# The rotary embedding's transfers on another engine's queue, and the key latent's norm at a later place

## The chip, the cores and the metric

One core of a Trainium2 chip runs the kernel as one program. The metric is the device time of one execution in microseconds. Times are the median of several runs; the profile is one execution taken by the hardware profiler. Five engines have instruction queues of their own and run in order within each: TensorE (PE; its weight loads are shown apart as PEld), VectorE (DVE), ScalarE (ACT), GpSimd (POOL) and SyncE (SP). A transfer is issued by the queue of some engine (shown as SPq or ACTq) and then carried out by the core's 16 DMA engines.

## The reference

Two layers of a decoder trunk over 512 tokens of width 1024, batch 1, all in float32. Each layer normalises its input, projects it with one wide matrix, and feeds three branches: a Mamba-2 state space model, multi-head latent attention (MLA), and a gated delta network. The branches are projected, gated and merged, and a feed-forward block follows. Only the attention branch matters here, in the reference's words:

```python
q = (rmsnorm(cq, q_norm_g) @ w_uq).reshape(Bsz, S, H, MLA_NOPE + MLA_ROPE)
q_nope, q_pe = jnp.split(q, [MLA_NOPE], axis=-1)
q_pe = apply_rope(q_pe, cos[:, :, None, :], sin[:, :, None, :])
kv = (rmsnorm(ckv, kv_norm_g) @ w_ukv).reshape(Bsz, S, H, MLA_NOPE + MLA_V)
k_nope, v = jnp.split(kv, [MLA_NOPE], axis=-1)
k_pe = apply_rope(k_rope, cos, sin)
```

There are 8 heads with 128 plain and 64 rotary columns. The query latent `cq` has 512 columns, the key latent `ckv` 256, and one rotary key of 64 columns serves all heads. `apply_rope` turns the first and second half of the 64 columns into t1 cos - t2 sin and t2 cos + t1 sin. Scores are the sum of the plain and the rotary product; a causal softmax and the product with v follow.

## The kernel before

**Precision.** TensorE multiplies in a rounded format, so each float32 operand is split into a high part (the rounded value) and a low part (the rest), and each product is three matmuls: high x high, high x low, low x high (`mm3`, L180 to L184). The split of a weight tile is a cast on ScalarE (`whi`, L154; L557 and L558 for the query weights) and a subtraction on VectorE (`wlo`, L155; L559 and L560). The split of an evicted result is likewise an operation of ScalarE (L250, L254) and one of VectorE (L251, L255).

**Weights.** They are streamed from HBM by SyncE into the two buffers of `wraw` (L161; L549 for the query weights), 384 or 512 KB at a time. A load is issued when the splits of the load two before are done. The split tiles `whi` and `wlo` have four buffers each, so a cast waits for the matmuls that use the tile four before.

**Order of the work.** The program is written as straight Python; a scheduler then orders the instructions of all engines, mostly as written, with some blocks given a priority. So the place of a statement in the source decides, with its waits, where its instructions stand in each engine's queue. Tiles with the tag `mix` rotate through eight buffers, and one that is written again waits for the last reader of the tile eight before.

**The attention stage of a layer.** A first projection has left the key latent in `ck_tok` (four tiles of 128 tokens x 256) and the rotary key in `kr_tok`. Then, in source order:

- `query_latent(0)` (L494): columns 0 to 255 of the query latent, transposed by construction, as two tiles, evicted with the gain and split (`cqh`, `cql`), and squared (L499, L501).
- `latent(...)` (L472): the key latent's norm and split. ScalarE squares and sums each of the four token tiles (L478). VectorE scales and adds the epsilon (L258), GpSimd raises to the power -1/2 (L259), VectorE multiplies (L482), TensorE transposes eight 128x128 blocks (L487), and the result is split with the gain into `ckh` and `ckl` (L254, L255).
- The rotary key: four transposes (L518), a copy (L520), `rope` (L503), and the split into `kph` and `kps` (L524 to L526).
- `query_latent(1)` (L528): columns 256 to 511 of the query latent.
- The query's norm factors, from column sums (L531).
- Four head pairs (hp 0 to 3). Each computes the queries from `cqh` and `cql` (three tiles: plain queries of two heads, and `qp`, the rotary columns of both; L580), calls `rope(qp)`, swaps its halves through `qd` (L585) and splits into `qps` and `qpl` (casts L589 and L591, subtraction L590). It computes keys (`kh`, `kl`) and values (`vh`, `vl`) from `ckh` and `ckl`, and then for each of the two heads the scores (L622 to L627, of which L625 and L626 are the rotary part), the softmax (L634, L635), transposes (L645) and the product with the values (L661 to L663).

**Transfers of the rotary part.** `rope` needs the tile with its 32-row blocks exchanged in pairs, and moves them within the on-chip memory by four transfers of 64 KB (L507); L585 exchanges the two 64-row halves by two transfers of 128 KB. All these are issued by ScalarE's queue. With five calls of `rope` and four of L585 in each of two layers they are 40 and 16 transfers.

Of the kernel before, what the change touches and what calls it, by code (L numbers as in the profile page):

```python
# [55 lines left out]
def hybrid_kernel(ctx, tc, a, out, depth=2, taps=None):  # L56
    nc = tc.nc
    pe, act, dve, pool, sync = nc.tensor, nc.scalar, nc.vector, nc.gpsimd, nc.sync
    uid = itertools.count()

    def mk(pl, shape, dt, tag, bufs=None):
        return pl.tile(shape, dt, tag=tag, name=f"{tag}_{next(uid)}", bufs=bufs)
# [19 lines left out]
    lp = ctx.enter_context(tc.tile_pool(name="lp", bufs=1))  # L82
# [10 lines left out]
    def sm_bank():  # L93
        return mk(ps_sm, [P, 512], F32, "sm")
# [70 lines left out]
    def weights(w2d, c0, n, K, hold=None, raw0=None):  # L165

        kt = min(1024 // n, K // P)  # L170
        step = 512 // n
        for k0 in range(0, K // P, kt):
            given = raw0 is not None and k0 == 0
            raw = raw0 if given else weights_raw(w2d, c0, n, k0, kt)
            for q in range(0, kt, step):
                hi, lo = split_half(raw[:, q * n : (q + step) * n], hold and hold[k0 + q], not given)
                v = lambda x: x.rearrange("p (k n) -> p k n", n=n)
                yield k0 + q, v(hi), v(lo)
# [7 lines left out]
    def dense_F(gen, cols, K, xh, xl, mid=None, banks=None, after=None):  # L186

        pss = banks or [acc_bank() for _ in cols]
        last = K // P - 1
        if mid:
            gen = list(gen)
            for i, hf in enumerate(HALVES):
                for ps, c in zip(pss, cols):
                    for k0, wh, wl in gen:
                        for k in range(wh.shape[1]):  # L200
                            kk = k0 + k
                            mm3(ps[:, hf], wh[:, k, c], wl[:, k, c], xh[kk][:, hf], xl[kk][:, hf], kk == 0, kk == last)
                if i == 0:
                    mid()
            return pss
        for k0, wh, wl in gen:
            for ps, c in zip(pss, cols):
                for k in range(wh.shape[1]):
                    a_, b_ = wh[:, k, c], wl[:, k, c]
                    mm3(ps[: a_.shape[1], :], a_, b_, xh[k0 + k], xl[k0 + k], k0 + k == 0, k0 + k == last)  # L210
            if after:
                after()
        return pss

    def tiles(n):
        return [slice(i, i + P) for i in range(0, n, P)]
# [36 lines left out]
    def split_gain(hi, lo, ps, g):  # L253
        act.activation(hi, ps, AF.Copy, scale=g)  # L254
        dve.scalar_tensor_tensor(lo, ps, g, f32(hi), ALU.mult, ALU.subtract)  # L255

    def rsq(o, ss, scale, eps, exp=None):
        dve.tensor_scalar(o, ss, scale, eps, ALU.mult, ALU.add)  # L258
        pool.tensor_tensor(o, o, (exp if exp is not None else nhalf)[:, : o.shape[1]], ALU.pow)  # L259
# [5 lines left out]
    def hilo_tags(pl, base, n=KD, w=S):  # L265
        return ([mk(pl, [P, w], F32R, f"{base}h{k}") for k in range(n)],
                [mk(pl, [P, w], F32R, f"{base}l{k}") for k in range(n)])
# [83 lines left out]
    for ly in range(depth):  # L351
# [5 lines left out]
        sconv_b, g_n1, g_ssd, g_q, g_kv, g_gdn, g_n2 = 0, 12, 20, 28, 32, 34, 35  # L357
# [3 lines left out]
        ck_tok = [mk(lp, [P, 256], F32, f"yh{4 + t}") for t in range(T)]  # L361
# [110 lines left out]
        def latent(pl, tok, width, gi, nm):  # L472

            nk = width // P
            ss = mk(sp, [P, T], F32, "lss")
            for t in range(T):
                jk = mk(ml, [P, width], F32, "pn3", 2)
                act.activation(jk, tok[t], AF.Square, accum_out=ss[:, t : t + 1])  # L478
            rs = mk(sp, [P, T], F32, "lrs")
            rsq(rs, ss, 1.0 / width, EPS)  # L480
            for t in range(T):
                dve.tensor_scalar(tok[t], tok[t], rs[:, t : t + 1], None, ALU.mult)  # L482
            hs, ls = hilo_tags(pl, nm, nk)
            for k in range(nk):
                ps = sm_bank()
                for t in range(T):
                    pe.transpose(ps[:, t * P : (t + 1) * P], tok[t][:, k * P : (k + 1) * P], ident)  # L487
                split_gain(hs[k], ls[k], ps, col(gi + k))
            return hs, ls
# [4 lines left out]
        def query_latent(i):  # L494
            for j, ps in enumerate(dense_F(weights(w_in, O_CQ + 256 * i, 256, D), tiles(256), D, xh, xl)):
                k = 2 * i + j
                split_gain(cqh[k], cql[k], ps, col(g_q + k))
                cq_sq.append(mk(ml, [P, S], F32, "pn3", 2))
                act.activation(cq_sq[-1], ps, AF.Square)  # L499
                if k:  # L500
                    dve.tensor_tensor(cq_sq[0], cq_sq[0], cq_sq[k], ALU.add)  # L501

        def rope(src):  # L503

            sw_ = mk(lp, [P, S], F32, "mix", 8)
            for i in range(4):
                act.dma_start(sw_[32 * i : 32 * i + 32], src[32 * (i ^ 1) : 32 * (i ^ 1) + 32])  # L507
            ta = mk(lp, [P, S], F32, "mix", 8)
            dve.tensor_tensor(ta, src, cosT, ALU.mult)
            dve.tensor_tensor(sw_, sw_, sinT, ALU.mult)  # L510
            dve.tensor_tensor(ta, ta, sw_, ALU.add)
            return ta

        query_latent(0)
        ckh, ckl = latent(lp, ck_tok, 256, g_kv, "ck")
        ps = sm_bank()
        for t in range(T):
            pe.transpose(ps[:, t * P : (t + 1) * P], kr_tok[:, t], ident)  # L518
        kd = mk(lp, [P, S], F32, "mix", 8)
        act.copy(kd, ps)  # L520
        kpe = rope(kd)
        kph = mk(ml, [P, S], F32R, "kph")
        kps = mk(ml, [P, S], F32R, "kps")
# [2 lines left out]
        dve.tensor_tensor(kps[64:], kpe[64:], f32(kph[64:]), ALU.subtract)  # L526

        query_latent(1)  # L528
        ps = sm_bank()
        for t in range(T):  # L530
            pe.matmul(ps[:, t : t + 1], cq_sq[0][:, t * P : (t + 1) * P], ones[:, 0:1], start=True, stop=True)  # L531
# [13 lines left out]
        for hp in range(4):  # L545
# [33 lines left out]
            qp = mk(ml, [P, S], F32, "qp")  # L579
            act.mul(qp, pp, scale)  # L580
            qr = rope(qp)

            qd = mk(lp, [P, S], F32, "mix", 8)
            for i in range(2):
                act.dma_start(qd[64 * i : 64 * i + 64], qr[64 * (1 - i) : 64 * (1 - i) + 64])  # L585
            qps = [mk(ml, [P, S], F32R, f"qps{j}") for j in range(2)]
            for j in range(2):
                half, other = (slice(64 * i, 64 * i + 64) for i in (j, 1 - j))
# [715 lines left out]
```

## Time and profile before

| | us |
|---|---|
| median of 3 runs | 2334.94 (2334.29 to 2338.41) |
| the profiled execution | 2335.61 |
| its span in the trace | 2333.8 |
| TensorE busy in the span | 2290.0 |
| VectorE busy | 1585.9 |
| ScalarE busy | 1177.4 |
| 384 KB query weight load, issue to landing (median) | 3.3 |
| 512 KB key/value weight load, issue to landing (median) | 3.7 |
| rotary transfer of 64 KB (L507), issue to landing (median) | 2.0 |
| rotary transfer of 128 KB (L585), issue to landing (median) | 2.3 |

The granted TensorE clock of the profiled execution was 0.996. In rows of the timeline the first number is the start in us from the span's start, the second the duration in us from the first start to the last end of the row's instructions (their number is after the x), and the bracket gives the idle time of that engine before the row and what ended it. A name such as `mix<-qp` is output<-input. Neighbouring matmuls overlap in the trace, so their pace is read from start to start.

### The profile page before, as it was taken

Reading aid. Unit: us, or ns where it says so; the run is one execution under the profiler, and the core shown is the slowest. Engines: PE = TensorE matmul, PEld = TensorE weight load, DVE = VectorE, ACT = ScalarE, POOL = GpSimd, SP = SyncE. Lnnn points to the kernel's source line nnn. Section 1 sums busy time; section 2 is a strip of 40 time slices with the busy share of each in tenths; the row PEclk is TensorE's granted clock in tenths of the full one; section 3 lists DMA queues with packets and bytes.
Section 4 is the critical chain, followed back from the end, with each engine's and each line's share of the span. In section 5 each row is a group of like instructions: output and inputs, shape, how many; then the busy total and the mean of one; then the engine's idle time right before and its main releaser. Section 6 shows DMA issues by size and latency. Waiting matters only on the chain.

```text
span 2333.8 us, 32026 instructions
## 1 busy us (share of the span) xinstructions
PE 2290.0 (98%) x11814; PEld 1884.8 (81%) x11814; DVE 1585.9 (68%) x3116; ACT 1177.4 (50%) x2455; POOL 59.1 (3%) x74
## 2 busy tenths in 40 slices
PE   8999999999999999999999999999999999999998
PEld 7878788878887888888887787888788878888886
DVE  7776666775665458767867765667656645677668
ACT  6666644333443345554656667443334434545545
POOL 0000000000000000000000000000000000000000
PEclk9999999999999999999999999999999999999999
DMA  4223533442222443233132235334422224333231
GB/s 136 83 73 91 171 100 109 122 132 79 80 78 69 148 144 109 74 116 118 51 97 72 74 99 163 105 103 140 115 83 85 68 80 155 127 117 100 91 109 46
DMA packets 208702, 239.85 MB, mean 103 GB/s; under 512 B 33888, under 2 KB 157472, under 8 KB 208544
## 3 DMA queue, kind: packets, MB, share of 16 engines
q1 hardware_dynamic: 205344, 233.07, 33.0%
q10 hardware_dynamic: 3200, 4.72, 0.8%
q8 instruction: 93, 1.52, 0.3%
q14 instruction: 65, 0.53, 0.1%
HBM read 221.41 MB, written 11.63 MB: 100 GB/s over the span
## 4 chain that ended last, share of the span: by engine, by line
PE 88%; DVE 6%; DMA 2%; ACT 2%; POOL 1%; issue 1%; ACTq 0%; SPq 0%; DVEq 0%; POOLq 0%
PE acc L182 23%; PE acc L183 22%; PE acc L184 22%; PE sm L182 2%; PE sm L184 2%; PE sm L183 2%; DVE wlo L155 1%; PE sm L742 1%; DMA eE<-d_c 1%; PE sm L645 1%; DVE tok L858 1%; DVE gQ L857 1%; PE sm L1015 1%; POOL gms L259 1%; PE yt L661 1%
## 5 line engine op out<-in xcount | busy, mean ns | idle before, releaser
L155 DVE TENSOR_TENSOR wlo<-wraw,whi 128x512 fp32r<-128x512 f32 (+1 forms) x552 | 376.5, 686 | 421.7 <-ACT whi L154 407.1
L154 ACT CAST whi<-wraw 128x512 fp32r<-128x512 f32 (+1 forms) x552 | 339.9, 618 | 593.4 <-PE acc L183 384.2
L184 PE MATMUL acc<-xh,wlo 128*128 128x512 f32 (+1 forms) x1248 | 486.3, 390 | 0.0
L182 PE MATMUL acc<-xh,whi 128*128 128x512 f32 (+1 forms) x1248 | 486.0, 390 | 0.0
L183 PE MATMUL acc<-xl,whi 128*128 128x512 f32 (+1 forms) x1248 | 484.6, 389 | 1.0 <-issue 1.0
L184 PEld LDWEIGHTS acc<-xh,wlo 128*128 128x128 f32 x1248 | 235.6, 189 | 45.7 <-issue 1.2
L183 PEld LDWEIGHTS acc<-xl,whi 128*128 128x128 f32 x1248 | 235.7, 189 | 44.2 <-DVE xl L255 0.4
L182 PEld LDWEIGHTS acc<-xh,whi 128*128 128x128 f32 x1248 | 235.2, 189 | 43.7 <-ACT xh L254 0.4
L182 PE MATMUL acc<-yh,whi 128*128 128x512 f32 x384 | 151.9, 399 | 0.0
L183 PE MATMUL acc<-yl,whi 128*128 128x512 f32 x384 | 151.4, 394 | 0.0
L184 PE MATMUL acc<-yh,wlo 128*128 128x512 f32 x384 | 151.2, 394 | 0.0
L686 DVE SCALAR_TENSOR_TENSOR ckl<-acc,pc,ckl 128x511 f32<-128x511 f32 (+2 forms) x168 | 120.2, 743 | 15.5 <-ACT ckl L682 8.2
L154 ACT CAST whi<-wr 128x512 fp32r<-128x512 f32 x128 | 79.5, 621 | 66.6 <-PE acc L184 30.3
L184 PE MATMUL acc<-whi,xl 128*128 128x512 f32 (+1 forms) x288 | 111.3, 386 | 0.0
L183 PE MATMUL acc<-wlo,xh 128*128 128x512 f32 (+1 forms) x288 | 111.1, 386 | 0.0
L182 PE MATMUL acc<-whi,xh 128*128 128x512 f32 (+1 forms) x288 | 110.3, 385 | 0.0
L182 PE MATMUL acc<-whi,yh 128*128 128x512 f32 x256 | 99.7, 390 | 0.0
L184 PE MATMUL acc<-whi,yl 128*128 128x512 f32 x256 | 99.7, 389 | 0.0
L183 PE MATMUL acc<-wlo,yh 128*128 128x512 f32 x256 | 99.6, 389 | 0.0
L155 DVE TENSOR_TENSOR wlo<-wr,whi 128x512 fp32r<-128x512 f32 x128 | 86.0, 685 | 12.2 <-ACT whi L154 11.6
L182 PEld LDWEIGHTS acc<-yh,whi 128*128 128x128 f32 x384 | 71.7, 188 | 16.8 <-ACT yh L254 1.7
L183 PEld LDWEIGHTS acc<-yl,whi 128*128 128x128 f32 x384 | 72.2, 188 | 15.2 <-issue 1.0
(418 smaller groups left out, 4520.9 us busy)
## 6 DMA issues: line engine op xcount, KB each, us to landing
wraw<-in_w_in_dram SPq DMA_DIRECT2D x144, 512.0 KB, 3.6
wraw<-in_w_up_dram SPq DMA_DIRECT2D x64, 512.0 KB, 3.6
wr<-in_w_down_dram SPq DMA_DIRECT2D x32, 1024.0 KB, 5.0
eE<-d_c SPq DMA_DIRECT2D x48, 256.0 KB, 4.0
wraw<-in_w_mla_out_dram SPq DMA_DIRECT2D x16, 512.0 KB, 3.4
eE<-d_e SPq DMA_DIRECT2D x32, 256.0 KB, 3.1
wraw<-in_w_ssd_out_dram SPq DMA_DIRECT2D x16, 512.0 KB, 3.4
wraw<-in_w_gdn_out_dram SPq DMA_DIRECT2D x16, 512.0 KB, 3.4
```

The source lines that it names most:

```text
L154: act.copy(hi, raw)
L155: dve.tensor_tensor(lo, raw, f32(hi), ALU.subtract)
L182: pe.matmul(o, ah, bh, start=start, stop=False, skip_group_check=more)
L183: pe.matmul(o, ah, bl, start=False, stop=False, skip_group_check=more)
L184: pe.matmul(o, al, bh, start=False, stop=stop, skip_group_check=more)
L259: pool.tensor_tensor(o, o, (exp if exp is not None else nhalf)[:, : o.shape[1]], ALU.pow)
L645: pe.transpose(ps[:, n : n + P], pn[t][:, kb * P : (kb + 1) * P], ident)
L661: pe.matmul(o, v_h, th[:, c : c + w], start=kb == 0, stop=False)
L686: dve.scalar_tensor_tensor(acc[:, d:], ps[:, : S - d], taps_[3 - d], acc[:, d:], ALU.mult, ALU.add)
L742: pe.matmul(py[:, h * 64 : (h + 1) * 64], e2[h // 4][:, h % 4, :], xd[:, h * 64 : (h + 1) * 64], start=True, stop=True)
L857: dve.tensor_tensor(pd, bc_last(nb[:, m, m + 1 :], m + 1), bc_mid(xb[:, m, : m + 1], 31 - m), ALU.mult)
L858: dve.tensor_tensor(xb[:, m + 1 :, : m + 1], xb[:, m + 1 :, : m + 1], pd, ALU.add)
```

## The change

The rotary transfers of L507 and L585 are issued by SyncE in place of ScalarE, and the call of `latent` stands behind `query_latent(1)` and no longer behind `query_latent(0)`, so the rotary key's transposes come directly after the first half of the query latent. Nothing else is edited.

```diff
             sw_ = mk(lp, [P, S], F32, "mix", 8)
             for i in range(4):
-                act.dma_start(sw_[32 * i : 32 * i + 32], src[32 * (i ^ 1) : 32 * (i ^ 1) + 32])
+                sync.dma_start(sw_[32 * i : 32 * i + 32], src[32 * (i ^ 1) : 32 * (i ^ 1) + 32])
...
         query_latent(0)
-        ckh, ckl = latent(lp, ck_tok, 256, g_kv, "ck")
         ps = sm_bank()
         for t in range(T):
             pe.transpose(ps[:, t * P : (t + 1) * P], kr_tok[:, t], ident)
...
         query_latent(1)
+        ckh, ckl = latent(lp, ck_tok, 256, g_kv, "ck")
         ps = sm_bank()
...
             qd = mk(lp, [P, S], F32, "mix", 8)
             for i in range(2):
-                act.dma_start(qd[64 * i : 64 * i + 64], qr[64 * (1 - i) : 64 * (1 - i) + 64])
+                sync.dma_start(qd[64 * i : 64 * i + 64], qr[64 * (1 - i) : 64 * (1 - i) + 64])
```

In the changed kernel L518 is L517, L520 is L519, and L524 to L526 are L523 to L525; L507 and L585 keep their numbers.

## The prediction

> **What bounds the kernel now.** I read the page's busy times first, then its chain, then the windows over the attention stages of both layers, and last the timeline of each idle time of TensorE in them.
>
> ```profile
> PE 2290.0 (98%) x11814; PEld 1884.8 (81%) x11814; DVE 1585.9 (68%) x3116; ACT 1177.4 (50%) x2455; POOL 59.1 (3%) x74
> PE 88%; DVE 6%; DMA 2%; ACT 2%; POOL 1%; issue 1%; ACTq 0%; SPq 0%; DVEq 0%; POOLq 0%
> ```
>
> TensorE is busy for 98% of the span and is 88% of the chain of waits. The change takes no matmul away (the built programs have the same ones), so it can win only idle time of TensorE. The order of the built instructions differs between the two kernels only in the latent-attention stage of each layer: about 43 to 200 us and 1199 to 1350 us of the span. Elsewhere every engine has the same sequence. The windows over these stretches, a little wider, end with their sums:
>
> ```profile
> sum 168.00, PE 163.87 PEld 133.48 DVE 133.12 ACT 112.62 POOL 2.06; mean PE 23.41 PEld 19.07 DVE 19.02 ACT 16.09 POOL 0.29
> sum 164.00, PE 157.69 PEld 129.70 DVE 119.97 ACT 104.52 POOL 2.13; mean PE 22.53 PEld 18.53 DVE 17.14 ACT 14.93 POOL 0.30
> ```
>
> 168.00 - 163.87 = 4.13 us idle in layer 0 and 164.00 - 157.69 = 6.31 us in layer 1: 10.4 us in all is the ceiling of any gain, 0.45% of the span. ScalarE (ACT) is busy for 112.62 of 168 us, so it isn't the bound; what counts is only where TensorE waits for it. These are the idle times, in brackets with their releaser:
>
> ```profile
> 54.16 0.44 PE L487 MATMUL sm<-ct,yh 128*128 128x128 f32 x2 [0.88 <-DVE yh L482]
> 82.20 0.50 PE L622 MATMUL sm<-kh,qh 128*128 128x512 f32 x1 [0.37 <-ACT pn L635]
> 144.30 0.39 PE L625 MATMUL sm<-kps,qps 128*128 128x256 f32 x1 [1.46 <-ACT qps L591]
> 152.65 0.50 PE L661 MATMUL yt<-mix,vh 128*128 128x512 f32 x1 [0.81 <-ACT mix L250]
> 153.58 0.50 PE L662 MATMUL yt<-mix,vh 128*128 128x512 f32 x1 [0.44 <-DVE mix L251]
> ...
> 1207.70 0.96 PE L487 MATMUL sm<-ct,yh 128*128 128x128 f32 x6 [1.33 <-DVE yh L482]
> 1230.29 0.47 PE L182 MATMUL acc<-cqh,whi 128*128 128x512 f32 x1 [0.21 <-DVE vl L251]
> 1238.30 0.39 PE L625 MATMUL sm<-kps,qps 128*128 128x256 f32 x1 [2.05 <-ACT qps L591]
> 1302.80 0.39 PE L625 MATMUL sm<-kps,qps 128*128 128x256 f32 x1 [1.31 <-ACT qps L591]
> 1311.15 0.49 PE L661 MATMUL yt<-mix,vh 128*128 128x512 f32 x1 [0.81 <-ACT mix L250]
> 1312.07 0.50 PE L662 MATMUL yt<-mix,vh 128*128 128x512 f32 x1 [0.43 <-DVE mix L251]
> ```
>
> They add up to 10.10 us, nearly the whole ceiling. Two belong to the key latent (L487: 0.88 + 1.33 = 2.21), three to the rotary part of the queries (L625 waiting for qps: 1.46 + 2.05 + 1.31 = 4.82), the rest to the softmax's and the values' evictions.
>
> **Part 1: 56 transfers leave ScalarE's queue for SyncE's.** What an issue costs ScalarE:
>
> ```profile
> L507 ACTq DMA_DIRECT2D mix<-qp x32: 514/601/1077, 68.3 to 1325.3; - x32
> L507 ACTq DMA_DIRECT2D mix<-mix x8: 551/610/621, 57.1 to 1212.6; - x8
> ...
> L585 ACTq DMA_DIRECT2D mix<-mix x16: 501/504/622, 74.8 to 1331.5; - x16
> ```
>
> 32 x 0.601 + 8 x 0.610 + 16 x 0.504 = 32.2 us of ScalarE's queue go. This hides behind TensorE's work except where a ScalarE result is late, so it isn't the gain. The three qps stalls are where it shows. The one of the third head pair, layer 0:
>
> ```profile
> 139.34 0.60 ACT L573 ACTIVATE qh<-acc 128x512 fp32r<-128x512 f32 x1 [0.96 <-PE acc L184]
> 139.93 1.15 ACTq L585 DMA_DIRECT2D mix<-mix  x2
> 141.18 0.62 ACT L154 CAST whi<-wraw 128x512 fp32r<-128x512 f32 x1 [1.24 <-PE acc L183]
> 141.70 1.26 ACT L589 CAST qps<-mix 64x512 fp32r<-64x512 f32 x2
> 142.99 1.26 ACT L591 CAST qps<-mix 64x512 fp32r<-64x512 f32 x2
> ```
>
> The two transfers of L585 can't be issued before the eviction of qh at 139.34, since they stand behind it on ScalarE; only then do the casts L589 and L591 run, and the matmul L625 starts at 144.30, 1.46 late. On SyncE L585 waits only for its data and its buffer, and is issued some 2 us earlier; the 1.15 us of issue is gone from ScalarE, so L589 (1.26) can run from about 139.95, ahead of the cast at 141.18. That cast waits for TensorE's progress and ends near 141.8; the first L591 (0.62) would end near 142.4, and L625 could start at 142.84 = 144.30 - 1.46. The margin is 0.4 us if the data land by 141.8. I take 1.46 - 0.3 = 1.16, and for the same place in layer 1, 1.31 - 0.3 = 1.01: the 0.3 is an estimate, most of the margin, for the landing beside a weight load.
>
> The largest stall, in the first head pair of layer 1:
>
> ```profile
> 1226.29 2.44 ACTq L507 DMA_DIRECT2D mix<-qp  x4
> 1231.82 1.15 ACTq L585 DMA_DIRECT2D mix<-mix  x2
> 1237.63 0.61 ACT L591 CAST qps<-mix 64x512 fp32r<-64x512 f32 x1 [2.71 <-DMA mix<-mix]
> 1232.26 0.37 SPq L161 DMA_DIRECT2D wraw<-in_mla_w_ukv_dram  x1
> 1233.29 0.37 SPq L549 DMA_DIRECT2D wraw<-in_mla_w_uq_dram  x1
> ```
>
> The four L507 block ScalarE for 2.44 us, the value evictions and casts behind them are late, and L585 goes out at 1231.82, when SyncE issues 512 KB at 1232.26 and 384 KB at 1233.29. The second of the two lands only at about 1237.6, and L625 waits 2.05. In the changed order the next pair's key/value load stands ahead of L585 on SyncE, but its wait is for two weight casts that no longer stand behind L507, so it goes out about 2.4 us earlier; L585 then follows it by over 1 us, and the following w_uq load is issued behind L585, not into it. I take all of the 2.05. The 0.21 at 1230.29 (late value evictions behind L507) goes too, and so does the 0.37 at 82.20.
>
> In the other five head pairs qps is no stall. The closest is the fourth of layer 0: L591 starts at 176.27 and its matmul at 176.97 without idle time.
>
> ```profile
> 172.45 1.15 ACTq L585 DMA_DIRECT2D mix<-mix  x2
> 176.27 0.62 ACT L591 CAST qps<-mix 64x512 fp32r<-64x512 f32 x1
> 176.97 0.37 PE L625 MATMUL sm<-kps,qps 128*128 128x256 f32 x1
> ...
> DMA to landing us min/median/max: 2.2/2.3/5.3
> ```
>
> With L585 issued at the same time (172.45) and the usual 2.3 us, it lands by 175.3 and nothing is late; with the 5.3 of the worst one it lands at 178.2, and L625 is about 2 us late. That bound is kept for the range. The median is nearest to seven of the eight pairs, so I cost it at nothing here.
>
> What the moved issues do to SyncE: it issues in order, so a weight load behind L507 or L585 waits for qp or for the rotated tile. An issue there takes 0.37 us (the rows at 1232.26 and 1233.29), 56 of them 20.7 us over 300 us: no bound. The key/value load of the next pair stands behind L507 in the first pair, the w_uq loads and d_c behind it in the second. They are needed a pair later, some 25 us on, and the wait of L507 is for an eviction that is nearly ready when SyncE gets there: nothing.
>
> In the trace the collision at 1232 was between two queues. The Trainium skill ("DMA: Bandwidth & Descriptors", section "Queues, rings and completion order") says that each DMA engine takes turns between the queue rows that have work, packet by packet, and within one row takes descriptors in order. That speaks against the change: a rotary transfer on SyncE would stand behind the whole of a load that it now shares turns with. No row of before shows a small transfer right behind a load on the same queue, so the trace neither bears it out nor refutes it; it is the last rival below.
>
> **Part 2: the key latent moves behind the query latent's second half.** It costs the same instructions at another place; what counts is whether its chain ends before TensorE arrives.
>
> ```profile
> 1203.76 0.42 ACT L478 ACTIVATE pn<-yh 128x256 f32<-128x256 f32 x1 [0.26 <-DVE pn L501]
> ...
> 1205.38 0.42 ACT L478 ACTIVATE pn<-yh 128x256 f32<-128x256 f32 x1
> 1205.92 0.17 DVE L258 TENSOR_SCALAR lrs<-lss 128x4 f32<-128x4 f32 x1 [1.67 <-ACT pn L478]
> 1207.29 1.14 DVE L482 TENSOR_SCALAR yh<-yh,lrs 128x256 f32<-128x256 f32 x4 [1.20 <-POOL lrs L259]
> ...
> 52.53 1.28 ACT L415 ACT_TABLE_LOAD   x1
> 56.48 0.39 PE L184 MATMUL acc<-xh,wlo 128*128 128x512 f32 x1
> 56.71 0.39 PE L182 MATMUL acc<-cqh,whi 128*128 128x512 f32 x1
> 1213.72 0.39 PE L182 MATMUL acc<-cqh,whi 128*128 128x512 f32 x1
> ```
>
> Four squares of 0.54 each (1203.76 to 1205.92) are 2.16 us, the norm's power on GpSimd 1.37 (1205.92 to 1207.29), and the transposes L487 start 0.41 later (1207.70): 3.94 us from the first square. In the changed order the transposes stand behind 32 of the first head pair's query matmuls, at about 0.227 us each (56.48 to 56.71 is one): 7.3 us after the query latent's end. The squares in turn stand on ScalarE behind the evictions of the query latent and five weight casts.
>
> Layer 0: the query latent, which now ends at 56.71, ends without the 0.88 us wait and without the eight transposes ahead of it (about 0.12 each, from 0.96 for six and 0.44 for two): 56.71 - 0.88 - 1.0 = 54.8. TensorE reaches L487 at 54.8 + 7.3 = 62.1. ScalarE has, from the eviction of the half's first tile near 53.6 on, that eviction and the next (0.6 each), the table load (1.28), two squares (0.6 each) and five casts (0.3 to 0.6): 5.9 us by these durations, so the latent's squares start near 59.4, an estimate, and L487 at 59.4 + 3.94 = 63.3: an idle time of 1.2 us in place of 0.88. Layer 1: 1213.72 - 1.33 - 1.0 = 1211.4, arrival 1218.7; there a cast ahead of the squares waits for a matmul of the same stretch, 3.9 us after the query latent's end, which puts the first square at 1215.6 with that cast, and L487 at 1219.5: idle 0.8 in place of 1.33. So 2.0 us in place of 2.21: the stall moves and stays; I cost the move at nothing. Bounds: the whole 2.21 is won if the casts go faster, and 2 us are lost if the eviction of ckh, which then stands behind a cast of the next pair's first w_uq load, has to wait for that load.
>
> The two idle pairs at the third head pair's end (0.81 + 0.44, 0.81 + 0.43) shrink: two 128x256 matmuls of about 0.12 now stand between, 0.24 each, 0.48 in all.
>
> **The sum.** Gains: 1.16 + 1.01 + 2.05 + 0.21 + 0.37 + 0.48 = 5.28; less 1.0 us, an estimate, for rotary transfers that land behind a load at one of the two places with little margin (half of the 2 us above). Net 4.3 us. The profiled execution took 2335.61 us, span 2333.8: 2335.61 - 4.3 = **2331.3 us**. The median of the runs, 2334.94, is 0.67 below the profiled one; I don't subtract that, as the spread of the runs (2334.29 to 2338.41) is larger.
>
> **Rivals.** (a) The latent's stall is gone as well, because ScalarE, free of 32 us of issues, finishes the squares earlier, and no landing is late: 5.28 + 2.21 = 7.5, 2328.1 us. For it: ScalarE is busy for only 67% here. Against: its squares wait for casts that follow TensorE, not for issues. (b) The change doesn't do what it says: the qps stalls are set by the casts' wait for TensorE (the row at 141.18 has 1.24 of it), and come back at L625 in another form: only 0.21 + 0.37 + 0.48 is won, 2334.6 us. (c) Slower: rotary transfers stand in one queue behind a 384 or 512 KB load and take 5.3 us like the worst one now. It decides once the landing passes about 3.5 us, the lead of the third and fourth pairs. Fourth pairs: 2 us late each, in both layers; third pairs: the stall stays and grows by 1.0; the first pair of layer 1 keeps 2.05; the latent loses 2 us on the late w_uq load. 2335.61 + 4.0 + 2.0 + 2.0 - 1.06 = 2342.6 us. By the skill's rule of turns between rows and order within one this is what comes; by the row at 1232, where the landing was 5.3 in a queue of its own, the place of a load matters, not the queue.
>
> **How the numbers follow.** Forecast 0.45 (2329.8 to 2333.0); (a) 0.25; (b) 0.12; (c) 0.18. A measurement of this kernel tells a change from none at about 0.2%, 4.7 us: faster is below 2330.3, slower above 2339.6. The forecast has a ninth of its weight below 2330.3: faster 0.05 + 0.25 = 0.30, plus 0.02 for the edges of (b); same 0.40 + 0.10; slower 0.18. The range reaches from (a) to a half-decided (c): 2327.5 to 2339.0, leaving out 0.05 below and 0.13 above.
>
> **What would show it.** Right: the queue q10 is gone; L507 and L585 stand on SPq at 0.37 each; no L625 row of the third pairs or of 1238 has more than 0.4 idle; L487 has about 1.2 and 0.8. Wrong: L585 landing above 3.5 us, an idle row at L625 in the fourth pairs, ckh's eviction waiting for a DMA, or L487 without idle time (rival a).

## The result, and the profile after

The changed kernel takes 2327.15 us (median of 9 runs, 2322.57 to 2335.17) against 2335.18 for the kernel before (9 runs, 2333.94 to 2338.41): a ratio of 0.9971, 95% interval 0.9961 to 0.9982. That is 4.2 to 9.1 us less. Six further runs gave 0.9968 (0.9955 to 0.9980). The forecast of -4.3 us had the sign and a place in the interval, but about half of the size; the median is just below the range's lower end. The runs of one kernel differ in granted clock (0.992 to 0.999), by about 1.7 us for each 0.001 (the slope over the 70 runs of the kernel before in these comparisons), so kernels are compared below by ratios over many runs and by what TensorE waits for in the two attention stages.

The page after, span, busy times and the transfers' one remaining queue:

```profile
span 2329.9 us, 32047 instructions
PE 2295.1 (99%) x11814; PEld 1891.3 (81%) x11814; DVE 1586.6 (68%) x3116; ACT 1177.7 (51%) x2455; POOL 59.2 (3%) x74
...
q1 hardware_dynamic: 208544, 237.80, 33.5%
```

ScalarE's queue q10 is gone; its 3200 packets are in q1 (205344 before). TensorE's busy time is 5.1 us more for the same matmuls, which fits this execution's lower clock (0.993 against 0.996). The same windows over the two stages as before the prediction end with these sums:

```profile
sum 168.00, PE 165.92 PEld 136.10 DVE 134.50 ACT 114.55 POOL 2.15; mean PE 23.70 PEld 19.44 DVE 19.21 ACT 16.36 POOL 0.31
sum 164.00, PE 161.49 PEld 132.65 DVE 125.21 ACT 109.24 POOL 2.14; mean PE 23.07 PEld 18.95 DVE 17.89 ACT 15.61 POOL 0.31
```

TensorE's idle time is 2.08 + 2.51 = 4.59 us, where it was 10.44. The timeline of TensorE shows what is left (the only rows over 0.2 us):

```profile
63.68 1.22 PE L487 MATMUL sm<-ct,yh 128*128 128x128 f32 x8 [1.11 <-DVE yh L482]
142.22 0.39 PE L625 MATMUL sm<-kps,qps 128*128 128x256 f32 x1 [0.21 <-ACT qps L591]
151.24 0.49 PE L661 MATMUL yt<-mix,vh 128*128 128x512 f32 x1 [0.29 <-ACT mix L250]
152.08 0.50 PE L662 MATMUL yt<-mix,vh 128*128 128x512 f32 x1 [0.35 <-DVE mix L251]
...
1218.18 1.23 PE L487 MATMUL sm<-ct,yh 128*128 128x128 f32 x8 [1.16 <-DVE yh L482]
1264.88 0.39 PE L625 MATMUL sm<-kps,qps 128*128 128x256 f32 x1 [0.53 <-ACT qps L591]
1304.75 0.49 PE L661 MATMUL yt<-mix,vh 128*128 128x512 f32 x1 [0.29 <-ACT mix L250]
1305.59 0.50 PE L662 MATMUL yt<-mix,vh 128*128 128x512 f32 x1 [0.35 <-DVE mix L251]
```

Read against the rows of before: L625's 4.82 us shrank to 0.74; L487's 2.21 became 2.27, so the latent's stall only moved; L661 and L662 shrank from 2.49 to 1.28. These lines account for 5.2 of the 5.85 us of idle time that went, the small rows of before (0.37 and 0.21) for the rest.

The profiled execution of the changed kernel doesn't show the whole gain in its span: 2329.9 against 2333.8 is 3.9 us less. Aligned matmul by matmul (both traces hold 11814), it was 6.5 us ahead of the kernel before at 1310 us and 6.7 at 1620, and fell to 3.4 by 1690, in code that is the same in both. The windows show why; the column before the DMA share is the granted clock. First after, then before:

```profile
55.00:80.00 25.00, 23.89 (x120) 19.76 (x119) 17.56 (x43) 17.37 (x46) 2.15 (x2) 0.93 0.24 74
480.00:520.00 40.00, 38.13 (x356) 30.53 (x354) 27.71 (x62) 14.78 (x26) 0.00 (x0) 0.87 0.51 132
1640.00:1680.00 40.00, 38.70 (x459) 31.09 (x458) 24.45 (x54) 17.04 (x29) 0.00 (x0) 0.87 0.48 120
```

```profile
55.00:80.00 25.00, 25.00 (x136) 20.85 (x135) 18.59 (x42) 14.89 (x37) 1.01 (x1) 1.00 0.34 97
480.00:520.00 40.00, 38.12 (x359) 30.89 (x358) 29.32 (x65) 15.09 (x25) 0.00 (x0) 0.89 0.52 136
1640.00:1680.00 40.00, 37.82 (x464) 30.69 (x463) 30.40 (x67) 15.86 (x27) 0.00 (x0) 1.00 0.51 133
```

The clock doesn't dip at the same places in every execution; here three dips more fell on the profile of after (the two shown, and one at 11 us). In another profile of the changed kernel no dip fell ahead of the last matmul. There the same matmuls of the attention stages, the 194th to the 1151st and the 5941st to the 7001st of the trace, took 2.94 and 4.58 us less than before: 7.5 us, near the 8.0 of the medians. I use this stage time below.

### The profile page after: what moved, and what is told of

Read it like the earlier page. It is cut to its first block, busy times and chain, and to the rows that moved or that the text cites. A ratio compares the mean times of both kernels' runs of the same rounds, so it can differ in the third digit from the quotient of the medians.

```text
span 2329.9 us, 32047 instructions
## 1 busy us (share of the span) xinstructions
PE 2295.1 (99%) x11814; PEld 1891.3 (81%) x11814; DVE 1586.6 (68%) x3116; ACT 1177.7 (51%) x2455; POOL 59.2 (3%) x74
## 4 chain that ended last, share of the span: by engine, by line
PE 89%; DVE 6%; DMA 2%; ACT 2%; POOL 1%; issue 1%; SPq 0%; DVEq 0%; POOLq 0%; ACTq 0%
PE acc L182 23%; PE acc L183 23%; PE acc L184 23%; PE sm L184 2%; PE sm L183 2%; PE sm L182 2%; DVE wlo L155 1%; PE sm L742 1%; DVE tok L858 1%; PE sm L645 1%; DVE gQ L857 1%; PE sm L1015 1%; POOL gms L259 1%; ACT whi L154 1%; PE yt L661 1%
```

## The experiments

Theory A was that of the prediction: the queue move brings nearly all of it, the latent's move nothing. Theory B was the opposite. After the first four runs both had fallen, and theories C and D took their place: C, that the two edits together give TensorE another order of instructions, with matmuls left as fillers, which run while an eviction is awaited; D, that the latent's later place itself frees ScalarE. In the table "idle" is TensorE's idle time in the windows of the two stages (10.44 before), and "stages" the change of the stage time.

| run | us, median | ratio to before (95%) | idle | stages |
|---|---|---|---|---|
| changed kernel again | 2327.89 | 0.9968 (0.9955 to 0.9980) | 5.06 | -7.5 |
| queue move alone | 2333.89 | 0.9995 (0.9985 to 1.0005) | 8.21 | -3.4 |
| latent's move alone | 2339.05 | 1.0020 (1.0010 to 1.0031) | 12.23 | +2.2 |
| latent's norm early | 2332.12 | 0.9985 (0.9974 to 0.9996) | 6.38 | -4.7 |
| queue move, no priority | 2323.05 | 0.9957 (0.9944 to 0.9970) | 3.31 | -9.7 |
| changed, no priority | 2321.87 | 0.9958 (0.9944 to 0.9971) | 4.00 | -8.6 |
| latent after the factors | 2331.46 | 0.9988 (0.9976 to 1.0000) | 5.83 | -5.4 |
| L585 back on ScalarE | 2325.24 | 0.9968 (0.9955 to 0.9981) | 5.23 | -8.4 |
| before, no priority | 2329.10 | 0.9982 (0.9971 to 0.9992) | 9.49 | -3.7 |
| norm early, no priority | 2322.23 | 0.9949 (0.9937 to 0.9961) | 2.13 | -11.3 |
| GpSimd's queue | 2331.59 | 0.9982 (0.9971 to 0.9993) | 6.83 | -4.9 |

Two of the stage times hold a dip of 3.4 us at half clock, worth 1.7 us by an estimate: without it the latent's move alone has +0.5 and GpSimd's queue -6.6.

### The changed kernel again

No edit.

> The changed kernel itself, beside the others on one chip. Theory A (the queue move brings nearly all of it, by ending the waits of the rotary scores for qps and ScalarE's late evictions) and theory B (the latent's later place brings most of it) both expect the 8.0 us again: 2324 to 2331 us against about 2335 before. If the granted clock makes the difference (0.992 to 0.998 in its runs so far), times of one clock should differ by less than 1 us, and 0.001 of clock by about 2.3 us.

It came to 2327.89 us, and 2321.01 at a clock of 0.999, where the kernel before has 2329.78 (the median of its 8 runs at that clock in all the comparisons here). The gain is real and isn't the clock's. But runs of one clock differ by more than the 1 us expected (at 0.998 the changed kernel took 2322.57, 2322.78 and 2326.47), and 0.001 of clock is worth 1.7 us, not 2.3.

### The queue move alone

```diff
-                act.dma_start(sw_[32 * i : 32 * i + 32], src[32 * (i ^ 1) : 32 * (i ^ 1) + 32])
+                sync.dma_start(sw_[32 * i : 32 * i + 32], src[32 * (i ^ 1) : 32 * (i ^ 1) + 32])
...
-                act.dma_start(qd[64 * i : 64 * i + 64], qr[64 * (1 - i) : 64 * (1 - i) + 64])
+                sync.dma_start(qd[64 * i : 64 * i + 64], qr[64 * (1 - i) : 64 * (1 - i) + 64])
```

> L507 and L585 issued by SyncE, the key latent at its old place. Theory A: 6 to 8 us below before, L625 idle rows under 0.5 each, the latent's two stalls of before (0.88 and 1.33) as they were. Theory B: at most 3 us below before.

2333.89, no change that can be measured in the whole time, though the stages of its profile are 3.4 us shorter: theory A falls. L625's waits do go down as it says (1.35 in all), but this timeline of TensorE shows others in their place:

```profile
81.12 0.39 PE L625 MATMUL sm<-kps,qps 128*128 128x256 f32 x1 [0.82 <-ACT qps L591]
98.87 0.55 PE L645 MATMUL sm<-ct,pn 128*128 128x128 f32 x3 [0.62 <-DVE pn L637]
...
149.80 0.28 PE L184 MATMUL acc<-whi,ckl 128*128 128x256 f32 x1
149.92 0.71 PE L645 MATMUL sm<-ct,pn 128*128 128x128 f32 x5
151.44 0.50 PE L661 MATMUL yt<-mix,vh 128*128 128x512 f32 x1 [0.81 <-ACT mix L250]
152.37 0.50 PE L662 MATMUL yt<-mix,vh 128*128 128x512 f32 x1 [0.43 <-DVE mix L251]
```

The third pair's last value matmul stands at 149.80, ahead of the five transposes; nothing is left to run while ScalarE and VectorE evict them, and L661 and L662 wait 1.24 us, as before the change. In the changed kernel two value matmuls stand behind the transposes (its rows are shown with the queue move without priority). The wait of L645 for the softmax (0.62, in both layers) is new.

### The latent's move alone

The call of `latent` behind `query_latent(1)`; L507 and L585 on ScalarE.

> The key latent at its new place, L507 and L585 issued by ScalarE as before. Theory A: within 1.5 us of before, with the qps stalls of the third head pairs still there and the latent's wait at L487 about 1.1 in each layer. Theory B: 4 us or more below before, with most of the qps stalls gone.

2339.05, slower by 0.1 to 0.3%: theory B falls as well. Most of the slowdown comes with a lower clock: its runs have 0.9945 in the mean, those of the kernel before beside them 0.9965, which at 1.7 us for each 0.001 is 3.4 of the 4.5 us between the medians (an estimate). Whether the program itself lowers the clock wasn't separated. The rows of L625 in its timeline:

```profile
80.10 0.39 PE L625 MATMUL sm<-kps,qps 128*128 128x256 f32 x1 [1.79 <-ACT qps L591]
144.56 0.39 PE L625 MATMUL sm<-kps,qps 128*128 128x256 f32 x1 [1.28 <-ACT qps L591]
1271.37 0.39 PE L625 MATMUL sm<-kps,qps 128*128 128x256 f32 x1 [1.10 <-ACT qps L591]
1303.88 0.45 PE L625 MATMUL sm<-kps,qps 128*128 128x256 f32 x1 [2.73 <-ACT qps L591]
```

6.9 us in all, 2.1 more than before. That ScalarE's own issues fall at worse places when the latent's evictions come later would explain it, but it wasn't followed row by row. So the two edits aren't additive: their stage times alone are -3.4 and +2.2 (some +0.5 without a clock dip of 0.83 over 1300 to 1310 us in that profile, by an estimate: 10 us x 0.17 = 1.7), and together -7.5.

### The latent's norm early

The changed kernel with `latent` cut in two:

```diff
         query_latent(0)
+        latent_norm(ck_tok, 256)
...
         query_latent(1)
         ckh, ckl = latent(lp, ck_tok, 256, g_kv, "ck")
```

`latent_norm` holds the loop of L478, the factors and L482; `latent` keeps the transposes and the split.

> The changed kernel, but the key latent's squares, factors and scaling (L478, L258, L482) stand at the old place behind the query latent's first half, and only its transposes and split at the new place. If the wait of L487 that is left in the changed kernel (1.11 and 1.16) is the chain from the squares to L482 being late, it goes, and the time is 2 to 2.5 us below the changed kernel's. If ScalarE is late again because the squares stand among the weight casts of the query latent, the idle time comes back elsewhere and the time is within 1 us of it.

The wait at L487 is gone, as expected; in its place the column sums (L531 of the changed kernel, L535 here) wait 0.83 and 0.62. But the time is 4 us above the changed kernel's (2.8 by the stage times), which neither branch of the expectation had. The end of the third head pair tells why (L665 and L666 here are L661 and L662):

```profile
151.22 0.49 PE L665 MATMUL yt<-mix,vh 128*128 128x512 f32 x1 [0.81 <-ACT mix L250]
152.15 0.50 PE L666 MATMUL yt<-mix,vh 128*128 128x512 f32 x1 [0.43 <-DVE mix L251]
```

The idle times are the queue move's. An edit 90 us earlier in the stage gave TensorE the queue move's sequence of matmuls again: by their names and shapes the two runs differ in the attention stages only up to 64 us in layer 0 and from 1195 to 1215 us in layer 1. This is what suggested theory C.

### The queue move without the keys' priority

The queue move alone, and:

```diff
-            with tc.high_priority(30):
+            with tc.high_priority(0):
                 ks = head_tiles(dense_F(wkv, [slice(0, P), slice(256, 256 + P)], 256, ckh, ckl), "k")
```

> The queue move alone (key latent at its old place), and the keys' matmuls and evictions lose their scheduling priority, so that in the built order value matmuls stand between the softmax's transposes and the product with the values in all head pairs. Theory C (the order of TensorE's instructions is what the two edits have together and neither alone: the matmuls that fill the eviction before L661 and L662 and before L645): the 2.88 us of idle time at L661 and L662 and the 1.34 at L645 of the queue move alone shrink by half or more, and the time comes 2 us or more below that of the queue move alone. Theory D (the latent's later place itself frees ScalarE in the first half of the stage): idle times as in the queue move alone, same time within 1 us.

2323.05 us, 11 below the queue move alone by the medians, 8.9 by the ratios, whose intervals are far apart, and 6.3 by the stage times. The latent is at its old place, so theory D falls; the idle time at L661, L662 and L645 went from 3.7 us (2 x 1.24 + 2 x 0.62) to 0.44 at one L645. Its third pair (another order, so other clock times):

```profile
145.77 0.38 PE L645 MATMUL sm<-ct,pn 128*128 128x128 f32 x2
145.91 0.48 PE L182 MATMUL acc<-ckh,whi 128*128 128x512 f32 x1
146.22 0.40 PE L183 MATMUL acc<-ckl,whi 128*128 128x512 f32 x1
146.46 0.40 PE L184 MATMUL acc<-ckh,wlo 128*128 128x512 f32 x1
146.77 0.49 PE L661 MATMUL yt<-mix,vh 128*128 128x512 f32 x1
147.10 0.29 PE L182 MATMUL acc<-whi,ckh 128*128 128x256 f32 x1
...
147.70 0.28 PE L184 MATMUL acc<-whi,ckl 128*128 128x256 f32 x1
147.82 0.39 PE L662 MATMUL yt<-mix,vh 128*128 128x512 f32 x1
```

Three key matmuls (128x512) stand ahead of L661 and six value matmuls (128x256) between L661 and L662, and no row has idle time. In the changed kernel two value matmuls stand at the same place:

```profile
150.00 0.71 PE L645 MATMUL sm<-ct,pn 128*128 128x128 f32 x5
150.47 0.36 PE L183 MATMUL acc<-wlo,ckh 128*128 128x256 f32 x1
150.67 0.28 PE L184 MATMUL acc<-whi,ckl 128*128 128x256 f32 x1
151.24 0.49 PE L661 MATMUL yt<-mix,vh 128*128 128x512 f32 x1 [0.29 <-ACT mix L250]
```

No filler, two value matmuls or three key matmuls ahead of L661 leave 0.81, 0.29 and no idle time. Their number alone doesn't set the wait: with L585 back on ScalarE (below) one value matmul stands there and L661 waits 0.16. The edit also changed the order on ScalarE and VectorE, and how much of the gain comes from these wasn't separated.

### The changed kernel without the keys' priority

The same line in the changed kernel.

> The changed kernel with the keys' priority taken away as well. Theory C: the order now has other fillers; wherever two or fewer matmuls stand before L661 the idle time comes back, the rest is as in the changed kernel: within 2 us of it either way. Theory D: no difference beyond 1 us, as the latent's place is the same.

2321.87; the interval overlaps the changed kernel's, and at 0.998 and 0.999 of clock the two differ by -0.7 and +0.7 us. No wait over 0.25 us is left at L661, L662 and L645, but L625 waits 1.40 at one place where it waited 0.21. Both theories allowed this; it doesn't tell them apart.

### The latent after the factors

`latent` one statement later, behind the `rsq` that follows L531.

> The key latent one statement later than in the changed kernel, behind the query's norm factors (L531), so its L487 stands behind the column sums. If the wait at L487 (1.11 and 1.16) is the squares' chain, it is not changed by one block of 0.8 us that itself waits for VectorE: L487 and L531 together wait about 1 us in each layer as now, and the time is within 1.5 us of the changed kernel's; the order of the third head pair's end is as in the changed kernel by theory C and so are its idle times.

A miss: 2331.46, 4 us above the changed kernel by the medians and 2.1 by the stage times. L487 does wait less (0.66 in layer 0, nothing over 0.15 in layer 1). But L625 waits 1.43 at 79.97, and in layer 1 the rows of L661 and L662 are back:

```profile
1306.42 0.50 PE L661 MATMUL yt<-mix,vh 128*128 128x512 f32 x1 [0.81 <-ACT mix L250]
1307.35 0.50 PE L662 MATMUL yt<-mix,vh 128*128 128x512 f32 x1 [0.43 <-DVE mix L251]
```

One statement is enough to lose a quarter of the gain by the stage times, half by the medians. It agrees with C in general; my expectation that this place of the order would stay was wrong for layer 1.

### L585 back on ScalarE

```diff
-                sync.dma_start(qd[64 * i : 64 * i + 64], qr[64 * (1 - i) : 64 * (1 - i) + 64])
+                act.dma_start(qd[64 * i : 64 * i + 64], qr[64 * (1 - i) : 64 * (1 - i) + 64])
```

> The changed kernel with L585 issued by ScalarE again (L507 stays on SyncE): 16 issues of 0.5 us return. If L507, with 2.44 us in a row, was what blocked ScalarE, the time is within 1.5 us of the changed kernel's; if L585's place behind the eviction of qh was (the third pairs' 1.46 and 1.31), these two stalls return and the time is 2 to 3 us above it.

2325.24, not above the changed kernel. The third pairs' waits return in part (1.17 and 0.76), and L661 and L662 shrink to 0.16 in each layer, so one pays for the other. L585's place on ScalarE does cost time at L625, then, and the order makes up for it. No run put L507 alone back, so what L507's 2.44 us in a row cost by themselves isn't shown.

### The kernel before without the keys' priority

> The kernel before with only the keys' scheduling priority taken away (the transfers stay on ScalarE, the latent at its old place). Theory C says that the order of TensorE's fillers and ScalarE's blocked queue are two separate causes: the 2.85 us at L661 and L662 of before shrink, the waits of L625 for qps (4.6 us in both layers) stay or grow, because ScalarE still issues; time 1 to 4 us below before, well above the queue move with the same edit (2323.05). If the order alone is what counts and the queue doesn't matter, it comes within 2 us of that one.

2329.10, 4.7 us below before by the medians and 4.2 by the ratio, at the upper end of what was expected, but not for the reason given: L661 and L662 still wait 0.81 and 0.44 (this order has no filler there either); what went is layer 1's 2.05 at L625. The third pairs' waits stay (1.46 in layer 0). It shows that this edit gives the fillers only together with the queue move, so what these fillers are worth with all transfers on ScalarE's queue stays open.

### The norm early without the keys' priority

> The norm of the key latent at the old place, its transposes at the new one, transfers on SyncE, and the keys' priority taken away. Where the norm early alone gave back at L661, L645 and the key matmuls what it won at L487, these now have fillers: idle time at L487 gone, 0.6 to 0.8 in each layer at L531 left, L661 and L645 small; 1 to 2 us below the queue move with the same edit (2323.05) if so. If the 1.3 at L531 and new waits eat it, the same within 1 us.

2322.23, the lowest ratio of all, 0.9949 (0.9937 to 0.9961); its interval overlaps the changed kernel's a little and that of the queue move without priority by more, so the 1 to 2 us expected between these two aren't shown. Idle time in the stages is 2.13 us, of which the rows at L535 are 0.85 and 0.64.

### GpSimd's queue

The changed kernel with `pool.dma_start` at L507 and L585.

> The changed kernel with L507 and L585 issued by GpSimd's queue, so that no rotary transfer stands behind a weight load or ahead of one on SyncE. If sharing SyncE's queue with the loads costs anything (rival c of the prediction in a small form), landings of L507 issued beside a load fall from 3.2 and the time falls by 0.5 us or more; if the load's traffic sets the landing whatever the queue, landings and time stay within 1 us, apart from what another order of TensorE's instructions does.

2331.59, 4 us above the changed kernel. L507's landings beside a load didn't fall: 3.8 at 152 us, where SyncE's had 3.3 (its median over all fell from 3.0 to 2.0, as fewer are issued beside a load). L625 waits for qps again at the third pairs (1.26 and 1.47), with L591 late for its data: the second transfer of L585 landed there in 4.3 and 4.5 us, beside a load that SyncE issued 0.2 us after the first. With L585 back on ScalarE it was 4.5 and 4.1, with a load 0.6 us after. On SyncE's own queue the load went out 1.8 and 1.2 us after, and it was 2.9 and 2.4. So at these places the shared queue kept the load back behind L585, and that was a help. How much of this is GpSimd's own queue and how much another order of TensorE wasn't separated.

## Why the prediction was half right

**The qps stalls (right).** Forecast: 4.22 of 4.82 us go. Measured: 4.08. The mechanism shows in ScalarE's timeline of the third pair after: L589 at 137.72, no longer behind the issue and the eviction of qh, which stands at 140.94 now. The reckoning of this place was luckier than it looks. It let L625 start behind the first L591, but in both traces L625 starts right behind the end of the second (144.25 before, 142.18 after); what made up for it is that the casts began 2.2 us ahead of the 139.95 assumed, because the eviction of qh moved behind L589.

```profile
137.72 1.26 ACT L589 CAST qps<-mix 64x512 fp32r<-64x512 f32 x2 [0.25 <-DVE mix L511]
139.00 0.62 ACT L154 CAST whi<-wraw 128x512 fp32r<-128x512 f32 x1
140.42 0.62 ACT L591 CAST qps<-mix 64x512 fp32r<-64x512 f32 x1 [0.79 <-DMA mix<-mix]
140.94 0.59 ACT L573 ACTIVATE qh<-acc 128x512 fp32r<-128x512 f32 x1
```

**The latent's stall (right).** Forecast 1.2 and 0.8 in place of 0.88 and 1.33; measured 1.11 and 1.16. In layer 0 the first square stands at 59.74 us where 59.4 was reckoned, so the chain behind the casts was the right one.

**Rotary transfers late behind a load (wrong size).** Rival (c) didn't come. Its bound of 5.3 us came from a transfer in a queue of its own. But late landings did cost something. The forecast had set 1.6 us aside for them (0.3 at each of the two third pairs, and 1.0); what is left at L625 is 0.74: 0.21 at 142.22, behind an L591 that had waited 0.79 for its transfer, and 0.53 at 1264.88 in the second pair of layer 1, where the forecast had no stall, behind this one:

```profile
1263.56 1.26 ACT L591 CAST qps<-mix 64x512 fp32r<-64x512 f32 x2 [1.28 <-DMA mix<-mix]
```

In the new queue L585 landed in 2.2 to 3.5 us. L507's median rose from 2.0 to 3.0 us, because six of its eight sets of four for `qp` now follow a 512 KB load by less than 0.5 us. TensorE hardly feels it: the four are issued 0.58 us apart, so a set has landed 4.5 to 5.3 us after its first issue, where one without a load takes 3.8. One set issued 0.46 us behind a 512 KB load landed in 3.2 (the six have 3.2 to 4.0); before, on ScalarE's queue beside a 512 KB load, one landed in 3.4 and the other in 4.2. The issues and landings in the stretch 96.5 to 100 us of after, then 130 to 135 us of before:

```profile
wraw<-in_mla_w_ukv_dram SPq DMA_DIRECT2D x1, 512.0 KB, 4.2
mix<-qp SPq DMA_DIRECT2D x4, 64.0 KB, 3.2
```

```profile
wraw<-in_w_in_dram SPq DMA_DIRECT2D x1, 512.0 KB, 4.1
mix<-qp ACTq DMA_DIRECT2D x4, 64.0 KB, 3.4
```

The load's company costs 1.2 to 2.2 us at the median (2.0 is the median of before), on either queue. The Trainium skill's rule of turns between queue rows and order within one ("DMA: Bandwidth & Descriptors", "Queues, rings and completion order") would have put the second case ahead; no run here shows that. The order within one row agrees with the trace: all 24 transfers of the six sets landed 0.2 to 1.8 us behind their load. But of the seven transfers of before that were issued beside such a load, in a queue of their own, six landed behind it as well. Another sentence of that page of the Trainium skill (section "Issuing engines are not separate DMA queues") fits better: more issuing engines only save the sequencer's time. Here it was ScalarE's time that was dear.

The prediction said that no row of before shows a small transfer right behind a load on the same queue. One does: SyncE issued a 128 KB read from HBM at 21.86 us, 0.43 behind a 512 KB load, and it landed in 4.2 us where the load took 4.3. It reads HBM, as the rotary transfers don't, but it was the nearest row at hand.

**The ends of the third pairs, and the rest of the order (the step that failed).** I took 0.48 us, from two fillers read off the built order; the rows gained 1.21, since the filler at L661 hides part of the eviction before L662 too. Worse, I costed each edit by the row that it touched and took the rest of the order as given. The experiments showed that any of these edits changes the order of the whole stage, and that this is worth more than the edits themselves: stage times of -3.4 and +2.2 (about +0.5 without its dip) apart, -7.5 together. The forecast came near because it was worked out on the order of the changed kernel, with both edits; by its own argument, which gives the queue all of it, the queue move alone should have gained as much, and it gained nothing that could be measured.

**The sum.** Idle time went down by 5.85 us where 4.3 were forecast; 0.9 of the difference is the landings, 0.7 the third pairs. In the second profile of the changed kernel idle time went down by 5.4 us (to 5.06) and the stage time by 7.5. The other 2.1 us are shorter steps between matmuls that the views count as busy; they weren't followed to a cause. So the ceiling "idle time of TensorE" was too low an account as well: the norm early without priority has a stage time 11.3 us shorter, above the ceiling of 10.4.

**Costs that were nothing.** An issue of L507 takes SyncE 0.58 us at the median, not the 0.37 of a weight load, and no idle row of TensorE over 0.2 us waits for a weight. The fourth pairs' small margin held.

## What to carry to other kernels

Moving small transfers off a compute engine's queue pays only where that engine's next result is the one that TensorE waits for; find those rows first. Where a scheduler orders the instructions, judge an edit by the order that it gives downstream: look for what stands between a transpose and the matmul that needs its eviction, and try the edit with and without a change of priorities, since each alone can show nothing. Compare idle time by stage, because a dip of the clock can hide half of such a gain in one profile; and look at what follows a long wait of TensorE (next section).

## What the runs showed of the hardware

The granted clock of the same program on one core varied from 0.992 to 0.999 between executions. In the profiles it isn't spread evenly: it is 1.00 nearly everywhere, with stretches at half clock (0.50) of 3.4, 10.2 or 13.7 us that come and go at the same places of the program (near 510 us in the profiles of before and after, not in the second profile of after; at 1662.9 us only in the first of after).

The traces show more of this than was used above. In the 13 profiles 15 such stretches fall ahead of the last matmul, and each begins within 2.1 us behind an idle time of TensorE of 1.1 to 2.7 us: in the profile of after at 65.5 us behind the 1.11 us of L487, in that of the latent's move alone at 1304.1 behind the 2.73 of L625. Most idle times that long are followed by none (84 of 99), and what decides between them wasn't found; nor was it tried whether the idle time is the cause. If it is, a wait of over 1 us can cost some 1.7 us more (an estimate: half of 3.4), and clock and idle time aren't separate accounts.

A transfer of 64 or 128 KB within the on-chip memory holds the queue that issues it for 0.5 to 0.6 us on ScalarE, SyncE and GpSimd alike (medians 0.60, 0.58 and 0.50 for L507), while a weight load of 384 or 512 KB holds SyncE for 0.37.
